# A corner of 64x64 triangular inverses: its first product moved from TensorE into VectorE's substitution

## The chip, the cores and the metric

One Trainium2 chip, of which the kernel uses one core. The metric is device time in microseconds of one execution of the whole layer, as the median of several runs. The engines are named as the profile names them: PE is TensorE (matmuls), DVE is VectorE, ACT is ScalarE, POOL is GpSimd, SP is SyncE, from which nearly all DMAs are issued.

## The reference

One layer of a hybrid encoder over 256 frames of width 4096, in float32. A projection of x feeds 16 heads of forgetting attention ("fox"), 32 heads of RWKV-7 time mixing (64 wide), and a gate; the gated outputs go through an output projection and a layer norm.

```python
proj = jnp.einsum('bsd,dc->bsc', x, w_in)
...
def frame_step(state, inp):
    r_t, w_t, k_t, v_t, a_t, b_t = inp
    sa = jnp.einsum('bhvk,bhk->bhv', state, a_t)
    state = (state * w_t[:, :, None, :] + sa[..., None] * b_t[:, :, None, :]
             + v_t[..., None] * k_t[:, :, None, :])
    return state, jnp.einsum('bhvk,bhk->bhv', state, r_t)
...
h = jnp.concatenate([fox_out, rwkv_out], axis=-1) * jax.nn.silu(z.astype(f32))
out = jnp.einsum('bsc,cd->bsd', h.astype(x.dtype), w_out)
x = _layernorm(ALPHA * x.astype(f32) + out.astype(f32), ln_gain, ln_bias, LN_EPS).astype(x.dtype)
```

The recurrence over frames is what the change touches. The kernel doesn't step through frames: it takes chunks of 64 frames (four of them), and inside a chunk the frames' influence on each other is the inverse of a unit triangular 64x64 matrix, one for each head and chunk.

## The kernel before, in words

**The main stream.** The two big projections run on PE as matmuls of 128x128 weights by 512 columns. Each float32 weight tile (128 x 1024) is loaded to `wr` (six buffers) and split into a rounded part, made by ACT (`wh`, four buffers), and the rest, made by DVE (`wl`, three buffers); lines 519 to 524. A tile of weights gives 12 matmuls: two pieces, two halves of the frames, three products each. First come 32 blocks of the input projection (n = 0 to 7 groups of two columns of heads, b = 0 to 3; lines 1311 to 1344), then eight blocks of the output projection (lines 1346 to 1392). Its first 32 weight tiles run on those heads that are already done (`begun`, line 600); then come the tiles 14 and 15 of block 0, which need the last heads' h, among them three that are not stored to memory and read back but kept in the tile `hl`.

**The side work.** While the main stream runs, generators (`prepare`, `rwkv`, `fox`, `unload`) are advanced one step after every second matmul triple (`slot`, line 592). `rwkv(n)` (line 918) does the time mixing of group n, that is four heads (two columns u, two halves j of the partitions) by four chunks c:

- `gp`: the products of the keys and receptances, masked into `gb` (the chunk's matrices, line 951) and `lt`.
- The 32x32 diagonal blocks of the triangular matrices are written to DRAM (`nd`) and read back spread over all partitions (`Nb`, line 955).
- The solve (lines 989 to 1001): DVE inverts all 32x32 blocks by back substitution, 31 steps of one product (`prod`) and one reduction (`xc`). A partition holds four columns (NJ = 4) of an inverse for each u; the width of a step grows from 1 to 31.
- The results go to DRAM (`td`) and come back as `T`, with blocks on their own partitions (lines 1002 to 1007); DVE transposes them into the diagonal of X (line 1026).
- The corner of each 64x64 inverse is a product of three 32x32 matrices. PE makes the first product `qt` from `gb` and T (lines 1027 to 1032, 16 matmuls, each two passes, 32 in the profile's count), ACT and DVE copy it to Q, and PE makes the second, `xp`, from Q and X (lines 1054 to 1059); ACT and DVE copy that into X.
- For each chunk: residual `rh`, solution `up`, state `sp` (lines 1068 to 1095), then the readout `yp` (lines 1096 to 1101): for each chunk and u, state SV by `lt` plus UV by `gb`, for both halves.
- `post`, norm and gate follow, and give h, which is stored or kept.

**What sets the order.** No engine's order is written by hand. `Later` (line 216) collects all operations with a modelled duration (`span_of`, line 149), and `flush` (line 274) runs them through a model of the five engines: each engine takes the ready operation with the lowest key, which is its place in the program, less 100000 for weight loads and splits (line 634). The order in the model becomes the program's order on each queue, and the engines then run in that order, waiting on semaphores. An operation counts as ready in the model some time after those that it depends on: `seen` (line 407) adds a margin of 1000 ns where PE depends on another engine, 1.5 times that behind a DMA and 0.15 times that otherwise (the margin is given with the flush, line 1374). `places` (line 418) looks whether the buffers of an operation's tiles are free in the model, and from when.

**Constants.** `cs` holds the 128x128 identity (C_ID), the masks, the right-hand sides of the solve (C_E) and others, for the whole run; the identity is needed in the end alone (lines 1381 and 1438).

Of the kernel before, what the change touches and what calls it, by code (L numbers as in the profile page):

```python
# [19 lines left out]
P = 128  # L20
S = 256
# [36 lines left out]
NJ = B // NG  # L58
C_ID = 0
C_MASK = 128  # L60
C_E = 256
C_SCAN = 384
C_ROW = C_SCAN + S
C_W = C_ROW + 2
LW = 2 * LORA + NF
# [26 lines left out]
MARGIN = 1000  # L92
APART = 2.4


# [120 lines left out]
class Later:  # L216
# [190 lines left out]
    def seen(self, o, op, margin):  # L407
        if o.engine == op.engine == "tensor":
            return o.start + o.hold
        if op.main or op.key < 0:  # L410
            return o.end
        if op.engine == "tensor":
            return o.end + margin
        if isinstance(o.lag, tuple):
            return o.end + margin * 1.5
        return o.end + margin * 0.15

    def places(self, op):
        at = 0.0
        for where in op.touches:  # L420
            if self.left[where][3]:
                continue
            free, queue = self.slots[self.left[where][0]]
            if not free or (len(free) < 5 and queue[0] != where and not self.left[where][0].startswith("ps")):
                return None
            at = max(at, free[0])
        return at
# [38 lines left out]
def layer(ctx: ExitStack, tc: tile.TileContext, xt, xtok, w_first, w_main, muv, w_o, up, par, mulora, fbias, lng, lnb, cst, out):  # L466
# [11 lines left out]

    cs = const.tile([P, C_W], F32, name="cs")
    prm = const.tile([P, len(PAR), G], F32, name="prm")  # L480
# [29 lines left out]
    nc.sync.dma_start(out=fb, in_=fbias)  # L510
    nc.sync.dma_start(out=cs, in_=cst)
    nc.earliest = 0

    ident = cs[:, C_ID : C_ID + P]

# [402 lines left out]
    def rwkv(n):  # L918
# [29 lines left out]
        for u in range(2):  # L948
            for j in range(2):
                h = HALF[j]  # L950
                nc.vector.tensor_tensor(gb[j][h, u], gv[u][j][h], m(h), ALU.mult)
            for a in range(4):
                o = B * (a % 2)
                nc.sync.dma_start(out=nd[u, a].rearrange("c r s -> r c s"), in_=gb[a // 2][B * a : B * (a + 1), u, :, o : o + B])
            nc.sync.dma_start(out=flat(nb[:, u]), in_=nd[u].rearrange("q c r s -> (q c) (r s)").unsqueeze(1).to_broadcast([16, NG, B * B]))
        for u in range(2):
            for j in range(2):
                o = HALF[1 - j]
                nc.vector.tensor_tensor(lt[j][o, u], parted(gv[u][j][o]), parted(m(o)), ALU.mult)
        states = rp.tile([P, 2, 2, NCH, C], F32, tag="SV", name=f"SV{n}")  # L960
        inputs = rp.tile([P, 2, 2, NCH, C], F32, tag="UV", name=f"UV{n}")
        SV, UV = ([t[:, j] for j in range(2)] for t in (states, inputs))
        yield from wait(W["tp"])
        for u in range(2):
            nc.vector.transpose(flat(BK[:, u]), flat(BK[:, u]))
        yield from wait(W["d1"])
        BKt = rp.tile([P, 2, NCH, P], F32, tag="shl", name=f"BKt{n}")
# [20 lines left out]
        other = turns()  # L988
        prod = rp.tile([P, 2, NJ, B], F32, tag="prod", name=f"prod{n}")
        xc = rp.tile([P, 2, NJ, B], F32, tag="xc", name=f"xc{n}")  # L990
        ev = cs[:, C_E : C_E + P].rearrange("p (j s) -> p j s", s=B)
        for u in range(2):
            nc.scalar.copy(prod[:, u], ev)
            nc.scalar.copy(xc[:, u, :, B - 1 : B], ev[:, :, B - 1 : B])
        for t, s in enumerate(range(B - 2, -1, -1)):
            w = B - 1 - s
            nc.vector.tensor_tensor(prod[:, :, :, s + 1 :], nb[:, :, s : s + 1, s + 1 :].to_broadcast([P, 2, NJ, w]), xc[:, :, :, s + 1 :], ALU.mult)
            nc.vector.tensor_reduce(xc[:, :, :, s : s + 1], prod[:, :, :, s:], AX.X, ALU.add)
            next(other, None)
            if t % ROWS == ROWS - 1:  # L1000
                yield
        td = dram.tile([2, 4, NCH, B, B], F32, tag="td", name=f"td{n}", bufs=2)
        T = rp.tile([P, 2, NCH, B], F32, tag="prod", name=f"T{n}")
        for u in range(2):
            nc.sync.dma_start(out=td[u].rearrange("q c (g j) s -> (q c g) (j s)", g=NG), in_=flat(xc[:, u]))
            for a in range(4):
                nc.sync.dma_start(out=T[B * a : B * (a + 1), u], in_=td[u, a].rearrange("c r s -> r c s"))
        vm = rp.tile([P, 2, 2, 2], F32, tag="vm", name=f"vm{n}")
# [14 lines left out]
        for a in range(4):  # L1023
            o = C * (a // 2) + B * (a % 2)
            rows = slice(B * a, B * (a + 1))
            nc.vector.transpose(X[rows].rearrange("p u c t -> p (u c) t")[:, :, o : o + B], T[rows].rearrange("p u c s -> p (u c) s"))
        qp = pst(f"qt{n}")
        for u in range(2):
            for c in range(NCH):
                for j in range(2):  # L1030
                    a, b = slice(C * j, C * j + B), slice(C * j + B, C * j + C)
                    nc.tensor.matmul(qp[b, u * P + c * B : u * P + (c + 1) * B], gb[j][a, u, c, B:C], T[a, u, c, :], start=True, stop=True)
        Q = rp.tile([P, 2, NCH, B], F32, tag="xc", name=f"Q{n}")
        for j in range(2):
            b = slice(C * j + B, C * j + C)
            (nc.vector.tensor_copy if j else nc.scalar.copy)(Q[b].rearrange("p u c s -> p (u c s)"), qp[b, : 2 * P])

        def residual(c):
# [13 lines left out]

        yield from wait(W["xp"])
        xp = pst(f"xp{n}")
# [42 lines left out]
        for c in range(NCH):  # L1097
            for u in range(2):
                for lhs, rhs in ((SV, [t[:, :, :, 1] for t in lt]), (UV, [t[:, :, :, C:P] for t in gb])):
                    for j in (1, 0):  # L1100
                        nc.tensor.matmul(yp[HALF[j], u * S + c * C : u * S + (c + 1) * C], lhs[j][:, u, c, :], rhs[j][:, u, c], start=lhs is SV, stop=lhs is UV)
        yield
# [245 lines left out]
    for b, q in outs:  # L1348
# [22 lines left out]
        if b == 0:  # L1371
            while sides:
                slot()
            nc.flush([t for _, *hl in ready for t in hl] + [raw for _, raw in raws], "_rp", MARGIN)
            mid.close()
            rpool = ctx.enter_context(tc.tile_pool(name="rpool", bufs=1))
            res = [rpool.tile([P, D], F32, tag=f"res{m}", name=f"res{m}") for m in range(2)]
            rows = rpool.tile([P, D], F32R, name="rows")
            nc.gpsimd.memset(rows.bitcast(F32), 0.0)
            identr = rpool.tile([P, P], F32R, name="identr")  # L1380
            nc.vector.tensor_copy(identr, ident)
            for n in range(2):
                load_tok(n)
            lbias = rpool.tile([P, OB], F32, name="lbias")
            lminus = rpool.tile([P, OB], F32, name="lminus")
            lneps = const.tile([P, 1], F32, name="lneps")
            nc.vector.memset(lneps, LN_EPS)
# [178 lines left out]
```

## Time and profile before

| | |
|---|---|
| runs before | 1906.97, 1906.69, 1906.51 us; median 1906.69 |
| the profiled execution | 1905.37 us; its span 1903.3 us |
| granted PE clock, mean | 0.999 |
| DVE, ACT, POOL busy | 1397.9, 970.8, 41.0 us |
| DMA | 443.89 MB in 349377 packets, 233 GB/s |
| qt of the eight groups, from the first to the last | 238.1 to 1555.1 us |
| yp, likewise | 272.1 to 1590.8 us |

Such rows are read so: engine, operation, the tile that it writes and those that it reads, partitions x elements, the count, then busy time and the mean duration of one, then the idle time of that engine just ahead of them and what ended it. In the rows of the timeline the first number is the start and the second the length, in us from the span's start. All operations have line 371, since the planner issues them there, so groups are told apart by tiles. Matmuls are pipelined: one begins while the one before it still runs, so the distance of two starts says what one costs.

### The profile page before, as it was taken

What the parts mean: (1) busy time and instruction counts of PE and PEld (TensorE: products, weight loads), DVE (VectorE), ACT (ScalarE), POOL (GpSimd) and SP (SyncE); (2) the same over time, 40 slices, a digit from 0 to 9 for tenths busy, and PEclk for the clock granted to TensorE, in tenths of its full rate; (3) what the DMA queues carried; (4) which work ended last, traced back from release to release, by engine and by line L of the source; (5) the groups of instructions that cost most, each with busy time, mean ns of one, the idle gap of its engine ahead of it and who ended that gap; (6) DMA issues with size and microseconds to landing.
All of it is one profiled execution on the core that took longest, in us unless ns stands there. A gap on an engine that the chain in (4) does not pass through costs nothing.

```text
span 1903.3 us, 28152 instructions
## 1 busy us (share of the span) xinstructions
PE 1894.5 (100%) x9882; PEld 1584.0 (83%) x9882; DVE 1397.9 (73%) x2413; ACT 970.8 (51%) x1488; POOL 41.0 (2%) x90
## 2 busy tenths in 40 slices
PE   9999999999999999999999999999999999999998
PEld 9988888888888888888888888888888888888887
DVE  6597778876887698769866986698669765765555
ACT  6464465445544554455445544554455444443342
POOL 0000000000000000000000000000000000000000
PEclk9999999999999999999999999999999999999999
DMA  9678877986897679777977798679767995966663
GB/s 349 212 220 261 228 206 241 262 225 193 241 261 227 199 233 265 229 199 229 270 226 198 234 264 225 195 239 267 225 196 231 340 306 174 318 206 200 190 197 144
DMA packets 349377, 443.89 MB, mean 233 GB/s; under 512 B 213666, under 2 KB 250116, under 8 KB 349236
## 3 DMA queue, kind: packets, MB, share of 16 engines
q1 hardware_dynamic: 348948, 441.73, 77.4%
q8 instruction: 77, 1.26, 0.3%
q14 instruction: 64, 0.52, 0.1%
q10 hardware_dynamic: 288, 0.37, 0.1%
HBM read 403.64 MB, written 38.36 MB: 232 GB/s over the span
## 4 chain that ended last, share of the span: by engine, by line
PE 99%; DVE 0%; DMA 0%; ACT 0%; issue 0%; DVEq 0%; SPq 0%; POOL 0%; ACTq 0%; POOLq 0%
PE acc L371 73%; PE oacc L371 18%; PE accl L371 2%; PE yp L371 1%; PE gp L371 1%; PE rh L371 1%; PE up L371 1%; PE lp L371 1%; PE sp L371 1%; PE fop L371 0%; PE fsp L371 0%; DMA fq<-bt 0%; PE side L371 0%; PE qt L371 0%; PE xp L371 0%; PE warmup L371 0%
## 5 line engine op out<-in xcount | busy, mean ns | idle before, releaser
L371 PE MATMUL acc<-w_1h,x 128*128 128x512 f32 x248 | 78.7, 394 | 0.0
L371 PE MATMUL acc<-w_0h,x 128*128 128x512 f32 x248 | 78.4, 393 | 0.2 <-ACT vt L371 0.2
L371 PE MATMUL acc<-w_8h,x 128*128 128x512 f32 x248 | 78.1, 392 | 0.0
L371 PE MATMUL acc<-w_5h,x 128*128 128x512 f32 x248 | 78.0, 392 | 0.0
L371 PE MATMUL acc<-w_15h,x 128*128 128x512 f32 x248 | 77.7, 394 | 0.0
L371 PE MATMUL acc<-w_13h,x 128*128 128x512 f32 x248 | 77.5, 392 | 0.0
L371 PE MATMUL acc<-w_10h,x 128*128 128x512 f32 x248 | 77.4, 393 | 0.0
L371 PE MATMUL acc<-w_9h,x 128*128 128x512 f32 x248 | 77.3, 392 | 0.0
L371 PE MATMUL acc<-w_14h,x 128*128 128x512 f32 x248 | 77.1, 391 | 0.0
L371 PE MATMUL acc<-w_3h,x 128*128 128x512 f32 x248 | 77.1, 392 | 0.0
L371 PE MATMUL acc<-w_11h,x 128*128 128x512 f32 x248 | 77.0, 392 | 0.0
L371 PE MATMUL acc<-w_12h,x 128*128 128x512 f32 x248 | 76.9, 391 | 0.0
L371 PE MATMUL acc<-w_2h,x 128*128 128x512 f32 x248 | 76.8, 390 | 0.0
L371 PE MATMUL acc<-w_6h,x 128*128 128x512 f32 x248 | 76.4, 389 | 0.0
L371 PE MATMUL acc<-w_4h,x 128*128 128x512 f32 x248 | 76.4, 389 | 0.0
L371 PE MATMUL acc<-w_7h,x 128*128 128x512 f32 x248 | 76.3, 389 | 0.0
L371 DVE TENSOR_REDUCE xc<-prod 128x8 f32<-128x16 f32 (+30 forms) x248 | 72.3, 291 | 5.5
L371 DVE TENSOR_TENSOR prod<-Nb,xc 128x8 f32<-128x8 f32 (+30 forms) x248 | 71.5, 288 | 6.3 <-DMA Nb<-nd 2.3
L371 DVE TENSOR_TENSOR w_7l<-w,w_7h 128x1024 fp32r<-128x1024 f32 x31 | 38.1, 1228 | 33.4 <-PE acc L371 31.2
L371 DVE TENSOR_TENSOR w_8l<-w,w_8h 128x1024 fp32r<-128x1024 f32 x31 | 38.0, 1225 | 31.2 <-PE acc L371 29.4
L371 ACT CAST w_11h<-w 128x1024 fp32r<-128x1024 f32 x31 | 32.7, 1055 | 48.6 <-PE acc L371 40.8
L371 ACT CAST w_10h<-w 128x1024 fp32r<-128x1024 f32 x31 | 32.7, 1055 | 47.2 <-PE acc L371 36.3
(652 smaller groups left out, 5451.6 us busy)
## 6 DMA issues: line engine op xcount, KB each, us to landing
w<-in_w_main_dram SPq DMA_DIRECT2D x496, 512.0 KB
wo<-in_w_o_dram SPq DMA_DIRECT2D x128, 512.0 KB
bt<-bk SPq DMA_DIRECT2D x96, 128.0 KB
fr<-in_w_first_dram SPq DMA_DIRECT2D x14, 720.0 KB
Nb<-nd SPq DMA_DIRECT2D x16, 512.0 KB
hd<-hl SPq DMA_DIRECT2D x29, 256.0 KB
h<-hd SPq DMA_DIRECT2D x29, 256.0 KB
raw<-bt SPq DMA_DIRECT2D x16, 256.0 KB
```

The costliest lines, as they stand in the source:

```text
L371: ins = op.call(*op.args, **op.kwargs)
```

## The change

1. **The corner's first product in the solve.** The off-diagonal 32x32 blocks of `gb` are transposed by DVE (`gt`), written to DRAM (`zd`) and read into the upper half of `prod`, which is twice as wide (2 NJ = 8 columns in place of four; the rest of that half is set to zero by POOL). They are right-hand sides of the same substitution: its 31 steps run over eight columns, and give, beside the inverses, the first products. These go through DRAM (`qd`) to Q, as the inverses go through `td` to T; T and Q now lie in one tile `TQ`, and T is loaded by four DMAs in place of eight. qt and its copies are gone, and so are the three steps of waiting ahead of xp.
2. **yp of chunk 0.** The state before the first chunk is zero in one half. ACT copies `lt` of chunk 0 into the half of `gb` that is otherwise zero, and the matmuls of SV for chunk 0 are left out: UV by `gb` does both.
3. **The identity** is no longer a part of `cs`, but is loaded to a tile of its own when the side work is done.
4. **The planner.** `seen` adds no margin where both operations are on the same engine (PE behind PE had none already). `places` lets an operation that writes a weight split (`wh`, `wl`) start no sooner than HOLD_OFF = 700 ns after its buffer is free, and counts several new tiles of one tag in one operation. The flush ahead of the output projection's second block keeps the accumulators of other blocks as taken.

```diff
-C_ID = 0
-C_MASK = 128
-C_E = 256
-C_SCAN = 384
+C_MASK = 0
+C_E = 128
+C_SCAN = 256
 C_ROW = C_SCAN + S
-C_W = C_ROW + 2
+C_ID = C_ROW + 2
+C_W = C_ID + P
...
+HOLD_OFF = 700
...
-        return o.end + margin * 0.15
+        return o.end + margin * 0.15 * (o.engine != op.engine)
...
-        at = 0.0
-        for where in op.touches:
-            if self.left[where][3]:
+        at, taken = 0.0, {}
+        for where in dict.fromkeys(op.touches):
+            tag, _, _, opened = self.left[where]
+            if opened:
                 continue
...
-            at = max(at, free[0])
+            at = max(at, free[n] + (HOLD_OFF if tag[:2] in ("wh", "wl") and op.engine != "tensor" else 0))
...
-    nc.sync.dma_start(out=cs, in_=cst)
+    nc.sync.dma_start(out=cs, in_=cst[:, :C_ID])
...
+            if u:
+                gt = rp.tile([P, 2 * NCH, B], F32, tag="xc", name=f"gt{n}")
+                zd = dram.tile([2, 2, NCH, B, B], F32, tag="zd", name=f"zd{n}", bufs=2)
+                for j in range(2):
+                    a = slice(C * j, C * j + B)
+                    nc.vector.transpose(gt[a], gb[j][a].rearrange("p u c t -> p (u c) t")[:, :, B:C])
+                    nc.sync.dma_start(out=zd[j].rearrange("u c k s -> k (u c) s"), in_=gt[a])
             nc.sync.dma_start(out=flat(nb[:, u]), in_=nd[u].rearrange("q c r s -> (q c) (r s)").unsqueeze(1).to_broadcast([16, NG, B * B]))
...
+        for j in range(2):
+            o = HALF[1 - j]
+            nc.scalar.copy(gb[j][o, :, 0, C:P], lt[j][o, :, 0, 1])
...
+        prod = rp.tile([P, 2, 2 * NJ, B], F32, tag="prod", name=f"prod{n}")
+        nc.gpsimd.memset(prod[:, :, NJ:], 0.0)
+        for j in range(2):
+            nc.sync.dma_start(out=prod[C * j : C * j + B, :, NJ:].rearrange("p u k s -> p u (k s)"), in_=zd[j].rearrange("u c (g k) s -> (c g) u (k s)", g=NG))
...
-            nc.vector.tensor_tensor(prod[:, :, :, s + 1 :], nb[:, :, s : s + 1, s + 1 :].to_broadcast([P, 2, NJ, w]), xc[:, :, :, s + 1 :], ALU.mult)
+            nc.vector.tensor_tensor(prod[:, :, :, s + 1 :], nb[:, :, s : s + 1, s + 1 :].to_broadcast([P, 2, 2 * NJ, w]), xc[:, :, :, s + 1 :], ALU.mult)
             nc.vector.tensor_reduce(xc[:, :, :, s : s + 1], prod[:, :, :, s:], AX.X, ALU.add)
...
-        td = dram.tile([2, 4, NCH, B, B], F32, tag="td", name=f"td{n}", bufs=2)
-        T = rp.tile([P, 2, NCH, B], F32, tag="prod", name=f"T{n}")
-        for u in range(2):
-            nc.sync.dma_start(out=td[u].rearrange("q c (g j) s -> (q c g) (j s)", g=NG), in_=flat(xc[:, u]))
-            for a in range(4):
-                nc.sync.dma_start(out=T[B * a : B * (a + 1), u], in_=td[u, a].rearrange("c r s -> r c s"))
+        td, qd = (dram.tile([4, 2, NCH, B, B], F32, tag=t, name=f"{t}{n}", bufs=2) for t in ("td", "qd"))
+        TQ = rp.tile([P, 2, 2 * NCH, B], F32, tag="prod", name=f"TQ{n}")
+        T, Q = (TQ[:, z].rearrange("p (u c) s -> p u c s", u=2) for z in range(2))
+        for d, cols in ((td, slice(0, NJ)), (qd, slice(NJ, 2 * NJ))):
+            for u in range(2):
+                nc.sync.dma_start(out=d[:, u].rearrange("q c (g j) s -> q (c g) (j s)", g=NG), in_=flat(xc[:, u, cols]))
+        for a in range(4):
+            nc.sync.dma_start(out=TQ[B * a : B * (a + 1), 0], in_=td[a].rearrange("u c r s -> r (u c) s"))
+        for j in range(2):
+            nc.sync.dma_start(out=TQ[C * j + B : C * j + C, 1], in_=qd[2 * j].rearrange("u c k s -> k (u c) s"))
...
-        qp = pst(f"qt{n}")
-        for u in range(2):
-            for c in range(NCH):
-                for j in range(2):
-                    a, b = slice(C * j, C * j + B), slice(C * j + B, C * j + C)
-                    nc.tensor.matmul(qp[b, u * P + c * B : u * P + (c + 1) * B], gb[j][a, u, c, B:C], T[a, u, c, :], start=True, stop=True)
-        Q = rp.tile([P, 2, NCH, B], F32, tag="xc", name=f"Q{n}")
-        for j in range(2):
-            b = slice(C * j + B, C * j + C)
-            (nc.vector.tensor_copy if j else nc.scalar.copy)(Q[b].rearrange("p u c s -> p (u c s)"), qp[b, : 2 * P])
...
-        yield from wait(W["xp"])
...
-                for lhs, rhs in ((SV, [t[:, :, :, 1] for t in lt]), (UV, [t[:, :, :, C:P] for t in gb])):
+                for lhs, rhs in ((SV, [t[:, :, :, 1] for t in lt]), (UV, [t[:, :, :, C:P] for t in gb]))[not c :]:
...
-            nc.flush([t for _, *hl in ready for t in hl] + [raw for _, raw in raws], "_rp", MARGIN)
+            nc.flush([t for _, *hl in ready for t in hl] + [raw for _, raw in raws] + [t for n in oacc if n for t in oacc[n]], "_rp", MARGIN)
...
+            ident = rpool.tile([P, P], F32, name="ident")
+            nc.sync.dma_start(out=ident, in_=cst[:, C_ID:])
             nc.vector.tensor_copy(identr, ident)
```

More of the change, by code (lines that the diff above doesn't have):

```diff
@@ L415, in seen @@
             return o.end + margin * 1.5
-        return o.end + margin * 0.15
+        return o.end + margin * 0.15 * (o.engine != op.engine)
     def places(self, op):
-        at = 0.0
-        for where in op.touches:
-            if self.left[where][3]:
+        at, taken = 0.0, {}
+        for where in dict.fromkeys(op.touches):
+            tag, _, _, opened = self.left[where]
+            if opened:
                 continue
-            free, queue = self.slots[self.left[where][0]]
-            if not free or (len(free) < 5 and queue[0] != where and not self.left[where][0].startswith("ps")):
+            free, queue = self.slots[tag]
+            n = taken[tag] = taken.get(tag, -1) + 1
+            if len(free) <= n or (len(free) < 5 and queue[n] != where and not tag.startswith("ps")):
                 return None
-            at = max(at, free[0])
+            at = max(at, free[n] + (HOLD_OFF if tag[:2] in ("wh", "wl") and op.engine != "tensor" else 0))
         return at
@@ L477, in pst @@
         return ps.tile([P, 512], F32, tag="ps", name=name)
-    cs = const.tile([P, C_W], F32, name="cs")
+    cs = const.tile([P, C_ID], F32, name="cs")
     prm = const.tile([P, len(PAR), G], F32, name="prm")
@@ L510, in layer @@
     nc.sync.dma_start(out=fb, in_=fbias)
-    nc.sync.dma_start(out=cs, in_=cst)
+    nc.sync.dma_start(out=cs, in_=cst[:, :C_ID])
     nc.earliest = 0
-    ident = cs[:, C_ID : C_ID + P]
     def column(name, i):
@@ L988, in rwkv @@
         other = turns()
-        prod = rp.tile([P, 2, NJ, B], F32, tag="prod", name=f"prod{n}")
-        xc = rp.tile([P, 2, NJ, B], F32, tag="xc", name=f"xc{n}")
+        xc = rp.tile([P, 2, 2 * NJ, B], F32, tag="xc", name=f"xc{n}")
         ev = cs[:, C_E : C_E + P].rearrange("p (j s) -> p j s", s=B)
         for u in range(2):
-            nc.scalar.copy(prod[:, u], ev)
-            nc.scalar.copy(xc[:, u, :, B - 1 : B], ev[:, :, B - 1 : B])
+            nc.scalar.copy(prod[:, u, :NJ], ev)
+            nc.scalar.copy(xc[:, u, :, B - 1 : B], prod[:, u, :, B - 1 : B])
         for t, s in enumerate(range(B - 2, -1, -1)):
             w = B - 1 - s
-            nc.vector.tensor_tensor(prod[:, :, :, s + 1 :], nb[:, :, s : s + 1, s + 1 :].to_broadcast([P, 2, NJ, w]), xc[:, :, :, s + 1 :], ALU.mult)
+            nc.vector.tensor_tensor(prod[:, :, :, s + 1 :], nb[:, :, s : s + 1, s + 1 :].to_broadcast([P, 2, 2 * NJ, w]), xc[:, :, :, s + 1 :], ALU.mult)
             nc.vector.tensor_reduce(xc[:, :, :, s : s + 1], prod[:, :, :, s:], AX.X, ALU.add)
@@ L1098, in rwkv @@
             for u in range(2):
-                for lhs, rhs in ((SV, [t[:, :, :, 1] for t in lt]), (UV, [t[:, :, :, C:P] for t in gb])):
+                for lhs, rhs in ((SV, [t[:, :, :, 1] for t in lt]), (UV, [t[:, :, :, C:P] for t in gb]))[not c :]:
                     for j in (1, 0):
-                        nc.tensor.matmul(yp[HALF[j], u * S + c * C : u * S + (c + 1) * C], lhs[j][:, u, c, :], rhs[j][:, u, c], start=lhs is SV, stop=lhs is UV)
+                        nc.tensor.matmul(yp[HALF[j], u * S + c * C : u * S + (c + 1) * C], lhs[j][:, u, c, :], rhs[j][:, u, c], start=lhs is SV or not c, stop=lhs is UV)
         yield
```

## The prediction

> **What bounds the kernel now.** I read the first page first (busy time, then the chain that ended last), then the waits of TensorE, then the busy time of one group's stretch.
>
> ```profile
> span 1903.3 us, 28152 instructions
> PE 1894.5 (100%) x9882; PEld 1584.0 (83%) x9882; DVE 1397.9 (73%) x2413; ACT 970.8 (51%) x1488; POOL 41.0 (2%) x90
> PE 99%; DVE 0%; DMA 0%; ACT 0%; issue 0%; DVEq 0%; SPq 0%; POOL 0%; ACTq 0%; POOLq 0%
> ```
> ```profile
> PE sp L371 <- ACT UV L371: 1.0, 1, 1.0
> ```
> ```profile
> 390.00:579.30 189.30, 189.30 (x1010) 157.31 (x1009) 145.59 (x265) 100.42 (x160) 4.44 (x9) 1.00 0.81 231
> ```
> TensorE is busy all but 8.8 us of the span, its longest wait is one of 1.0 us, and the chain that ended last is TensorE for 99%. The last row is one group (two columns of heads; there are eight): its columns are PE, PEld, DVE, ACT, POOL, granted clock, DMA share and GB/s. PE fills all 189.3 us, at full clock. So what leaves PE leaves the time, one for one, as long as nothing makes PE wait. DVE has 43.7 us free in a group, ACT 88.9 us, POOL nearly all. The profiled execution took 1905.37 us: its span and 2.07 us around it, 1.32 us less than the median of the runs, 1906.69.
>
> **What leaves PE.** Two things: the product qt, and the SV half of yp for the first chunk.
>
> ```profile
> L371 PE MATMUL yp<-lt,SV 128*64 128x64 f32 x256 | 15.8, 225 | 0.0
> L371 PE MATMUL qt<-T,gb 32*32 32x32 f32 x256 | 5.5, 192 | 0.0
> ```
> ```profile
> 237.29 0.39 PE L371 MATMUL acc<-w_12l,x 128*128 128x512 f32 x1
> 237.52 0.61 PE L371 MATMUL acc<-w_12h,x 128*128 128x512 f32 x2
> 238.07 0.69 PE L371 MATMUL qt<-T,gb 32*32 32x32 f32 x32
> 238.69 0.50 PE L371 MATMUL acc<-w_12l,x 128*128 128x512 f32 x1
> 239.03 0.62 PE L371 MATMUL acc<-w_12h,x 128*128 128x512 f32 x2
> 239.49 0.40 PE L371 MATMUL acc<-w_12l,x 128*128 128x512 f32 x1
> ```
> Matmuls overlap, so the price is read from starts, not from busy time. In the undisturbed rhythm (237.29 to 237.52) one weight matmul follows another by 0.23 us. From 237.52 to 239.03 three weight matmuls start; they are worth 0.69 us and it took 1.51. So a qt costs 0.82 us: 0.62 for its own 32 passes (238.07 to 238.69) and 0.20 at its edges. Eight of them: 6.6 us.
>
> ```profile
> 272.25 0.29 PE L371 MATMUL yp<-gb,UV 128*64 128x64 f32 x4
> 272.37 0.29 PE L371 MATMUL yp<-lt,SV 128*64 128x64 f32 x4
> 272.48 0.29 PE L371 MATMUL yp<-gb,UV 128*64 128x64 f32 x4
> ```
> The rows of yp (256 passes of the SV half in eight groups, so 32 a group) start 0.115 us apart, four passes each. For chunk 0 both SV rows go (u = 0 and 1): 2 x 0.115 x 8 = 1.9 us. No edge is won here, since yp stays. The UV half takes over the work of the missing one by two ACT copies of lt into the empty half of gb, far ahead of yp. Nothing new runs on PE. Sum: 6.6 + 1.9 = 8.5 us.
>
> **What DVE gets.** The substitution has 31 steps of a product and a reduction, and each is now twice as wide.
>
> ```profile
> L371 DVE TENSOR_REDUCE xc<-prod 128x8 f32<-128x16 f32 (+30 forms) x248 | 72.3, 291 | 5.5
> L371 DVE TENSOR_TENSOR prod<-Nb,xc 128x8 f32<-128x8 f32 (+30 forms) x248 | 71.5, 288 | 6.3 <-DMA Nb<-nd 2.3
> ```
> ```profile
> L371 DVE STREAM_TRANSPOSE X<-T 32x256 f32<-32x256 f32 x32 | 13.9, 435 | 0.8
> L371 DVE TENSOR_TENSOR prod<-Nb,xc 128x248 f32<-128x248 f32 x8 | 3.3, 416 | 0.2
> L371 DVE TENSOR_REDUCE xc<-prod 128x8 f32<-128x256 f32 x8 | 3.3, 415 | 0.0
> L371 DVE TENSOR_TENSOR prod<-Nb,xc 128x8 f32<-128x8 f32 x8 | 1.4, 172 | 2.3 <-DMA Nb<-nd 2.3
> L371 DVE TENSOR_REDUCE xc<-prod 128x8 f32<-128x16 f32 x8 | 1.1, 140 | 0.1
> ```
> From 8 to 248 elements a product grows from 172 to 416 ns, 1.02 ns an element; a reduction from 140 to 415 ns over 240 elements, 1.15. Step w adds 8w elements to the product and 8(w+1) to the reduction; over w = 1 to 31 that is 3968 and 4216 elements, so 4.0 + 4.8 = 8.9 us a group on top of today's 18.0 (143.8 in eight groups). The two transposes into gt add 2 x 0.435 us, and the copy of Q that goes saves about as much as one. So DVE takes some 9.3 us more of the 43.7 us that it has free: PE is not overtaken. ACT wins and loses copies of a few tenths of a us, POOL gets a memset; both have the room shown above.
>
> **Where it becomes later.** The solve is a chain, and on the way to yp. In one solve:
>
> ```profile
> 353.00:400.70 47.70, 41.26 (x94) 1.00 0.87 255
> ```
> ```profile
> 365.27 1.22 DVE L371 TENSOR_TENSOR w_8l<-w,w_8h 128x1024 fp32r<-128x1024 f32 x1 [0.49 <-PE acc L371]
> 367.30 0.27 DVE L371 TENSOR_REDUCE xc<-prod 128x8 f32<-128x112 f32 x1
> 367.99 1.23 DVE L371 TENSOR_TENSOR w_9l<-w,w_9h 128x1024 fp32r<-128x1024 f32 x1 [0.42 <-PE acc L371]
> ```
> ```profile
> 373.63 0.39 PE L371 MATMUL acc<-w_9l,x 128*128 128x512 f32 x1
> ```
> The first row (DVE alone) says: 41.3 us of work in 47.7, 6.4 us idle. The weight splits take 1.23 us in every 2.72, 45%, so what doesn't fit the idle time costs 1.82 us for each us of work. If all the idle time is filled, the solve gets (8.9 - 6.4) x 1.82 = 4.5 us longer; if none, 16.2. I take 6, near the low end, by the bracketed 0.42 and 0.49 us: DVE stands in front of a split whose buffer PE still reads, with the next step queued behind. HOLD_OFF plans each split 0.7 us later, so that steps go ahead of it. Besides, the planner no longer adds 0.15 us between two dependent steps on one engine; 62 steps times 0.15 us are 9.3 us of planned gaps, about what the wider steps add, so the planned order hardly stretches. A split that starts 0.7 us later still has cover: w_9l is done at 369.22 and first read at 373.63, 4.4 us later.
>
> The rest of that way:
>
> ```profile
> 241.18 0.69 PE L371 MATMUL xp<-X,Q 32*32 32x32 f32 x32
> ```
> ```profile
> 406.64 2.25 SPq L371 DMA_DIRECT2D T<-td  x3
> 410.33 3.28 SPq L371 DMA_DIRECT2D T<-td  x4
> 414.14 0.43 SPq L371 DMA_DIRECT2D T<-td  x1
> ```
> xp stands 3.1 us behind qt (238.07 to 241.18); of that, four transposes of X (1.7 us) are still needed, so 0 to 1.4 us is won; I take 0.5. SP issues 14 DMAs a group in place of 10 (zd and the load into prod ahead of the solve, qd and Q behind it; T in four in place of eight), past weight loads that are queued there. The eight T loads (128 pieces of 128 bytes each) took SP 7.9 us. zd writes and Q reads have as many pieces again, half of them behind the solve: 0 to 4.0 us ahead of it and 0 to 4.0 behind; I take 0.5 each, since T needs only half as many issues and zd goes while Nb is under way. So yp moves by 6 - 0.5 + 1 = 6.5 us (3.1 to 24.2).
>
> Who waits for that? In groups 0 to 6 nobody on PE. In the last group h does:
>
> ```profile
> 1621.88 0.42 DVE L371 TENSOR_TENSOR hl<-h,hl 128x256 fp32r<-128x256 f32 x1 [0.47 <-ACT hl L371]
> ```
> ```profile
> 1630.53 0.61 PE L371 MATMUL oacc<-wo_15h,hl 128*128 128x512 f32 x2
> ```
> The last hl is ready at 1622.30 and wo_15 needs it at 1630.53: 8.2 us of cover. The need comes 1.1 us sooner in the new kernel (this group's own qt and yp rows), so 7.2 are left, and the 6.5 us stay under it by 0.7. The move of ident to a tile of its own puts one load ahead of the identr cast in DVE's queue at the same place, and the splits behind it have the 4.4 us of lead as cover; I count it at nothing, or at most (that cover gone) the 1.0 us of the wait shown above. At most that 1.0 us is won back, too, if the wait on UV goes.
>
> By this the profiled execution would be 1905.37 - 8.5 = 1896.9 us, the median of the runs 1906.69 - 8.5 = **1898.2**; with the wait of 1.0 us lost or won, 1897.2 to 1899.2.
>
> **A rule against it.** The page's count of small packets says how common such pieces already are:
>
> ```profile
> DMA packets 349377, 443.89 MB, mean 233 GB/s; under 512 B 213666, under 2 KB 250116, under 8 KB 349236
> ```
> The change adds 1024 pieces of 128 bytes a group, 8192 in all, 4% of the 213666. The Trainium skill, "DMA: Bandwidth & Descriptors", section Specifications, says that transfers under 512 bytes don't run at line rate, since the engine reads, modifies and writes. By that rule the time would be the one of rival 2. No row here has the price of one such piece by itself, so the trace doesn't decide it.
>
> **The rivals.** (1) The late tail: the solve uses little of DVE's idle time and stretches by 9 to 16 us. For it: fixed queue order, DVE waits for PE in it. Against: the planned gaps that go. yp moves 9.5 to 16.5 us, PE stands 2.3 to 9.3 us before wo_15: 1900.5 to 1907.5; 1901.5 at 10.5 us.
> (2) Slow small pieces: zd and Q cost SP and the queue what T's cost, 4.0 us on each side of the solve. yp moves 6 - 0.5 + 8.0 = 13.5 us, PE waits 6.3: 1904.5. Against: the eight T loads are mostly spaced out by weight loads between them.
> (3) Slower: splits starve PE at the end of each solve. A step of the last dozen takes up to 0.67 + 0.71 us (416 + 248 x 1.02; 415 + 256 x 1.15). A tile of weights leaves DVE 2.72 - 1.23 = 1.49 us: two operations fit, three (2.06) don't, and the split comes 0.57 us later each time. Over eight tiles that is 4.6 us, just the lead of 4.4. With four between splits (2.75 us, six tiles) it is 7.6 us: PE would wait 3.2 us in each group, 25.6 in all, 1923.8. It turns slower once a group loses more than 1.5 us. Against: splits come first in the planner.
> (4) The change doesn't return qt's edges, because xp's group takes them over: 8 x 0.62 + 1.9 = 6.9 us, 1899.8.
>
> **How the numbers follow.** The forecast has 0.60, the late tail 0.17, the small pieces 0.06, starved splits 0.10, lost edges 0.07. A measurement of this kernel can tell about 0.2%, 3.8 us: faster is under 1902.9, slower above 1910.5. Forecast, lost edges and two thirds of the late tail are faster (0.78); the rest of the tail, the small pieces and half of the starved splits are the same (0.17); 0.05 are slower. The range goes from 1896.5, a little under the forecast's own low end, to 1905.0, which takes in rivals 2 and 4 and most of 1; starved splits and the long end of the tail stay out, some 0.15.
>
> **What would show it.** Right: no qt, 192 passes of the SV half of yp, PE's idle time still near 9 us, the product at 496 elements near 0.67 us, a solve of 52 to 56 us, hl ready some 1 us ahead of wo_15, and DVE near 1472 us. Wrong: a wait of PE for hl or h in the row of waits (rivals 1, 2), waits of weight matmuls for DVE's splits in every group (3), or weight matmuls still set back beside xp by more than now (4).

## The result, and the profile after

The changed kernel takes **1894.88 us** (median of five runs, 1894.52 to 1898.45), the kernel before 1906.97 (five runs, 1906.51 to 1908.25) in the same series: ratio 0.9938 [0.9926, 0.9949], or 9.7 to 14.1 us less. The forecast was 1898.2, its range 1896.5 to 1905.0: the sign was right, but the result lies 1.6 us below the low end. The profiled execution of the changed kernel took 1894.52 us, its span 1892.7.

The first page of the changed kernel:

```profile
span 1892.7 us, 27577 instructions
PE 1885.3 (100%) x9562; PEld 1577.5 (83%) x9562; DVE 1452.0 (77%) x2421; ACT 975.0 (52%) x1496; POOL 41.3 (2%) x98
DMA packets 360913, 446.49 MB, mean 236 GB/s; under 512 B 222002, under 2 KB 261652, under 8 KB 360772
```

TensorE still fills the span but for 7.4 us (8.8 before). All waits of TensorE in it that are long enough for the view:

```profile
PE warmup L372 <- POOL idle L372: 1.0, 1, 1.0
PE accl L372 <- ACT wf1h L372: 0.4, 1, 0.4
PE wp L372 <- ACT l L372: 0.2, 1, 0.2
```

The wait of sp for UV is gone, none came for a weight split, and none for h or hl. The substitution, in the groups of instructions:

```profile
L372 DVE TENSOR_TENSOR prod<-Nb,xc 128x16 f32<-128x16 f32 (+30 forms) x248 | 104.8, 423 | 13.6 <-ACT xc L372 7.9
L372 DVE TENSOR_REDUCE xc<-prod 128x16 f32<-128x32 f32 (+30 forms) x248 | 107.5, 434 | 4.5
```

104.8 + 107.5 against 71.5 + 72.3: 68.5 us more, 8.6 a group. One group to the next, read from the first matmul of the same weight tile in two consecutive groups of the changed kernel:

```profile
841.21 0.62 PE L372 MATMUL acc<-w_7h,x 128*128 128x512 f32 x2
...
1029.40 0.62 PE L372 MATMUL acc<-w_7h,x 128*128 128x512 f32 x2
```

1029.40 - 841.21 = 188.19 us. The same two starts lie 189.24 apart in the kernel before: a group is 1.05 us shorter.

The end of the side work in the changed kernel, in the timeline of VectorE and of TensorE:

```profile
1611.03 0.42 DVE L372 TENSOR_TENSOR hl<-h,hl 128x256 fp32r<-128x256 f32 x1
```
```profile
1620.51 0.62 PE L372 MATMUL oacc<-wo_15h,hl 128*128 128x512 f32 x2
```

The last hl is ready at 1611.45, 10.85 us sooner than before; wo_15 reads it 10.02 us sooner. The cover, 8.2 us before, is 9.1 now. The forecast had it down to 0.7.

### The profile page after: what moved, and what is told of

It is laid out like the page before. It is cut to its first block, busy times and chain, and to the rows that moved or that the text cites. A ratio compares the mean times of both kernels' runs of the same rounds, so it can differ in the third digit from the quotient of the medians.

```text
span 1892.7 us, 27577 instructions
## 1 busy us (share of the span) xinstructions
PE 1885.3 (100%) x9562; PEld 1577.5 (83%) x9562; DVE 1452.0 (77%) x2421; ACT 975.0 (52%) x1496; POOL 41.3 (2%) x98
## 2 busy tenths in 40 slices
DMA packets 360913, 446.49 MB, mean 236 GB/s; under 512 B 222002, under 2 KB 261652, under 8 KB 360772
## 4 chain that ended last, share of the span: by engine, by line
PE 99%; DVE 0%; DMA 0%; DVEq 0%; issue 0%; SPq 0%; ACT 0%
PE acc L372 73%; PE oacc L372 18%; PE accl L372 2%; PE gp L372 1%; PE yp L372 1%; PE rh L372 1%; PE up L372 1%; PE lp L372 1%; PE sp L372 1%; PE fop L372 1%; PE fsp L372 0%; PE side L372 0%; PE xp L372 0%; DMA fr<-in_w_first_dram 0%; DVE res L372 0%; PE wp L372 0%
## 5 line engine op out<-in xcount | busy, mean ns | idle before, releaser
L372 DVE TENSOR_TENSOR prod<-Nb,xc 128x16 f32<-128x16 f32 (+30 forms) x248 | 104.8, 423 | 13.6 <-ACT xc L372 7.9
L372 DVE TENSOR_REDUCE xc<-prod 128x16 f32<-128x32 f32 (+30 forms) x248 | 107.5, 434 | 4.5
L372 ACT CAST w_6h<-w 128x1024 fp32r<-128x1024 f32 x31 | 32.6, 1053 | 46.8 <-PE acc L372 43.7
L372 ACT CAST w_7h<-w 128x1024 fp32r<-128x1024 f32 x31 | 32.7, 1054 | 43.3 <-PE acc L372 39.9
L372 PEld LDWEIGHTS acc<-w_0h,x 128*128 128x128 f32 x248 | 46.6, 188 | 10.0 <-DVE vx L372 0.4
```

The source lines that it names most:

```text
L372: ins = op.call(*op.args, **op.kwargs)
```

## The experiments

The theory to test, A: TensorE's passes set the time, 1.05 us in each of eight groups, and everything else is cover that holds or doesn't. Its rivals: the new order of the queues wins by itself; the wider solve is nearly out of cover; the wait of sp for UV is worth more than the 1.0 us of one execution. In each diff the lines with a minus belong to the kernel named. Each ratio is to the kernel before, run in between on the same chip. There were three such series on three chips, in which the kernel before has medians of 1907.68, 1908.18 and 1908.86 us, so times of different series are best compared by their ratios.

### The order of the queues alone

The kernel before, with part 4 of the change (`seen`, `places`, the flush) and nothing else.

```diff
+HOLD_OFF = 700
...
-        return o.end + margin * 0.15
+        return o.end + margin * 0.15 * (o.engine != op.engine)
...
-            at = max(at, free[0])
+            at = max(at, free[n] + (HOLD_OFF if tag[:2] in ("wh", "wl") and op.engine != "tensor" else 0))
...
```

> The kernel before with the planner's edits alone (HOLD_OFF, no margin on the same engine, the places and the flush of after); qt, yp and the narrow solve stay. Theory A (PE time): nothing leaves PE, so the eight groups keep their 189.2 us each; at most the one wait of 1.0 us in the last group (sp for UV) goes. Time 1905.9 to 1907.0 us. Theory B (order): the new queues win the 3.6 us by which the change beat the forecast (12.1 instead of 8.5), with no matmul removed: about 1903.4 us, and groups shorter by some 0.4 us.

1908.14 us; ratio 0.9995 [0.9985, 1.0004]: no difference that can be told, a gain of 2.9 us at most. The waits of TensorE:

```profile
PE qt L372 <- DMA T<-td: 1.3, 1, 1.3
PE oacc L372 <- ACT bk L372: 0.5, 1, 0.5
```

The wait of sp is gone and two others have come. The order alone wins nothing in time. But it shortens the solve a lot, from 48.0 to 50.0 us to 35.1 to 36.8, of which more below.

### The edit of yp alone

The kernel before, with the two copies of lt into gb and the shorter list for chunk 0.

```diff
+            nc.scalar.copy(gb[j][o, :, 0, C:P], lt[j][o, :, 0, 1])
...
-                for lhs, rhs in ((SV, [...]), (UV, [...])):
+                for lhs, rhs in ((SV, [...]), (UV, [...]))[not c :]:
```

> The kernel before with only the SV half of yp for chunk 0 left out (lt copied into gb by ACT). Theory A: 64 of 512 passes go, 0.23 us a group, 1.9 us in all: 1905.1 us, each group 188.95 to 189.0 us. Rival: the passes of SV and UV overlap, so that a missing row of four returns less than the 0.115 us between starts: under 1 us in all, 1906 us or more.

1907.59 us; ratio 0.9993 [0.9982, 1.0004]. Inconclusive: 1.9 us are 0.9990, inside an interval that also holds 1. In the trace the groups without a stall are 189.04 us apart (189.24 before), 0.2 us less as the rows of yp said. But sp waits longer than in the first profile, and two more waits have come:

```profile
PE sp L371 <- ACT UV L371: 2.0, 1, 2.0
PE acc L371 <- ACT vt L371: 1.2, 4, 0.6
PE fsp L371 <- DVE qx L371: 1.0, 1, 1.0
```

### qt made twice

The kernel before, with the 16 matmuls of qt issued a second time right behind the first, into the same places.

> The kernel before with the 32 passes of qt issued twice in one group of matmuls (the second time overwrites the first with the same values). Theory A with edges paid once per group: 32 more passes cost 0.50 to 0.62 us a group, 4.0 to 5.0 us in all: 1911.0 to 1912.0 us. If the 0.20 us of edges belonged to the passes themselves: 0.82 us a group, 6.6 us: 1913.6 us. If small matmuls hid under the weight matmuls: under 1 us.

1912.09 us; ratio 1.0024 [1.0012, 1.0035], 4.4 us more by the medians. The groups are 189.82 us apart: 0.58 us for 32 more passes whose edges are paid already.

### The changed kernel once more

> The changed kernel once more, for a second profile. Theory A: each group again 1.05 us shorter than before, no wait of sp for UV in the last group, and what is left of the 12.1 us (the end behind the last matmul, 11.4 us against 11.9, and the difference between the profiled execution and the median) is spread between executions: the end anywhere from 11.3 to 11.9 us, the median 1894.5 to 1896 us. Theory B says nothing else here.

1895.14 us (five runs); ratio 0.9937 [0.9924, 0.9950]. The result stands. The groups without a stall are 188.2 us apart again. This profiled execution, at 1898.07 the slowest of its five, has three waits that the first one doesn't show:

```profile
PE fsp L372 <- DVE kx L372: 1.1, 1, 1.1
PE acc L372 <- ACT bk L372: 0.8, 1, 0.8
PE xp L372 <- DMA TQ<-qd: 0.5, 1, 0.5
```

So single waits of about a microsecond come and go between executions of one program.

### One load planned later

What does sp wait for? The timeline of ScalarE in the kernel before, last group:

```profile
1562.01 0.42 ACT L371 ACTIVATE fq<-fq 128x256 f32<-128x256 f32 x1 [2.72 <-DMA fq<-bt]
...
1563.55 1.03 ACT L371 CAST wo_0h<-wo 128x1024 fp32r<-128x1024 f32 x1
1564.48 0.53 ACT L371 COPY UV<-up 64x128 f32<-64x128 f32 x2
```

The bracket says that the scaling of fq, work of a fox head, stood 2.72 us for its load. The copy of UV, which needs nothing from it, stood behind it in the same queue, and TensorE behind the copy. The last matmul of up, which UV copies, ends at about 1561.5: some 0.5 us of the wait for the load held UV up directly, and the rest of its delay is the work between the two, which came late with the scaling. In the changed kernel UV is copied at 1550.80, ahead of that scaling. The experiment is the kernel before, in which the planner takes the last fox head's loads to land 4 us later, so that UV goes first:

```diff
+        if self.late:
+            op.lag = op.lag[0], op.lag[1] + self.late, op.lag[2]
...
+            nc.late = 4000 * (i == G - 1)
             issue(t, d[4 * j : 4 * j + 4].rearrange("b i m a t -> (b i) (m a t)"))
+            nc.late = 0
```

> The kernel before, with one change to the plan alone: the four loads of the last fox head count as landing 4 us later, so that in ACT's queue the copies of UV (first chunk of the last group) stand ahead of the scaling of fq, which waits for its load. Nothing leaves PE. Theory C: the forecast was beaten because the kernel before loses 1.2 to 2.8 us in the last group, where PE (sp) waits for UV behind fq, and the changed kernel does not. Then this wait is gone, no other takes its place, and the time falls by 1 to 3 us: 1904.7 to 1906.7 us against 1907.7 of before. Rival D: the waits are scattered and others (T, bk) come in its place, as in the kernel with the planner's edits alone: 1907.7 us, within 0.5.

1906.43 us against 1908.18; ratio 0.9987 [0.9978, 0.9996]: 0.8 to 4.2 us less, 1.75 by the medians. No wait of sp is left in its trace. So taking this wait away wins time, and by the medians more than the 1.0 us of the first profile; the interval reaches down to 0.8, so that it is more is likely and not shown.

### The changed kernel with an order near the old one

The changed kernel with HOLD_OFF = 0 and a margin of 100 ns between operations of one engine (150 in the kernel before; that full margin wasn't tried with the wider solve).

```diff
-HOLD_OFF = 700
+HOLD_OFF = 0
...
-        return o.end + margin * 0.15 * (o.engine != op.engine)
+        return o.end + margin * (0.15 if o.engine != op.engine else 0.1)
```

> The changed kernel with HOLD_OFF = 0 and a margin of 100 ns between operations on the same engine (150 before, 0 after). The corner and yp as after. Theory A and C: the PE time stays won, UV still stands ahead of fq in ACT's queue; the solve stretches from 51 to 53 us to 56 to 62 us, which the cover of the last group takes (hl ready 9.1 us ahead of wo_15 in the changed kernel). Time 1894.9 to 1897 us. Theory B: the order is worth the 3.6 us: 1898.7 us. Rival of the late tail: PE waits for hl by more than 1 us: 1897 us or more.

1907.76 us; ratio 0.9997 [0.9989, 1.0006]. All of the gain is gone, a larger loss than I expected of it. Waits of TensorE, then the busy time of VectorE in the last group's solve:

```profile
PE acc L372 <- DVE vx L372: 4.4, 6, 1.1
PE oacc L372 <- ACT hl L372: 2.1, 1, 2.1
PE xp L372 <- DMA TQ<-qd: 1.6, 1, 1.6
```
```profile
1494.00:1552.90 58.90, 52.09 (x97) 1.00 1.05 355
```

The solve leaves 6.8 us idle and takes 58.9 (56.9 to 58.9 in the eight groups), the last hl is ready at 1635.46, and TensorE waits 2.1 us for one of the last three. That is the late tail of the prediction, and beside it stands a wait for vx, six times, that no rival had.

### The corner without the edit of yp

The changed kernel with the two copies and the shorter list taken back.

> The changed kernel with the SV half of yp for chunk 0 back (and the two ACT copies gone). Theory A: 0.23 us more a group, 1.9 us in all: 1897.0 us, groups of 188.45 us in place of 188.2. If overlapped passes return less than their distance of starts: 1895.1 to 1896 us.

1899.48 us; ratio 0.9953 [0.9940, 0.9965], 4.6 us above the changed kernel's first median. The groups are 188.45 us apart, 0.26 more than with the edit, which makes 2.1 us in eight; the profile has also one wait of 1.1 us (oacc for the split wo_13l). In the clean groups, then, yp's term is what the rows said. The rest of the 4.6 isn't in the groups: that wait is a part of it, and so is the change of series, since against the kernel before beside it this kernel gains 8.7 us, and the changed kernel gained 12.1 and 12.5.

### A longer last solve

The changed kernel, with the product of each step of the last group's solve made twice: 13.1 us more for VectorE (an eighth of the 104.8 us above).

```diff
+            if n == G // 2 - 1 and w > 0:
+                nc.vector.tensor_tensor(prod[:, :, :, s + 1 :], nb[:, :, s : s + 1, s + 1 :].to_broadcast([P, 2, 2 * NJ, w]), xc[:, :, :, s + 1 :], ALU.mult)
```

> The changed kernel with each of the 31 products of the last group's solve made twice (same values): 13.1 us more of DVE work on the way to the last h, nothing more on PE. Theory of the forecast (only the last group's h has a reader on PE that can wait, behind 9.1 us of cover): the solve stretches by 13.1 to 23.8 us, and PE waits 4 to 14.7 us near wo_14 and wo_15: 1899 to 1910 us. Rival: the average share of DVE counts and the tail is hidden anyway: 1895 to 1896 us. With the changed kernel's own cover far larger than 9 us (other work moves ahead of it on PE), the same.

1911.18 us; ratio 1.0017 [1.0007, 1.0026]. The last solve takes 77.3 us instead of 50.6 (first product to last reduction): 26.7 more, twice the work that was added (the prediction's factor for a solve without idle time to fill, 1.82, makes 23.8). The wait of TensorE, and TensorE's busy time and granted clock in stretches ahead of it and behind it:

```profile
PE oacc L372 <- ACT hl L372: 11.9, 1, 11.9
```
```profile
1617.60:1619.60 2.00, 2.00 (x9) 1.00 0.79 219
1631.60:1633.60 2.00, 2.00 (x5) 0.50 0.00 0
```

So a solve that ends late does end the time, through hl, and the wait is paid with more than its length: see the last section.

### Which edit of the planner makes the fit

The changed kernel with HOLD_OFF = 0 alone (no margin between operations of one engine, as in the changed kernel), and with the margin of 100 ns on one engine alone.

> The changed kernel with HOLD_OFF = 0 and nothing else altered (the margin of 100 or 150 ns stays). Theory A, the two planner edits share the fit: solves of 53 to 57 us, one or two waits of acc for vx or of oacc for hl of 1 to 2 us, 1897 to 1904. Theory B, HOLD_OFF alone makes the fit: this run looks like e6, solves of 57 to 60 us, waits of acc for vx of 4 us, 1905 to 1909. Theory C, the margin alone makes it: solves of 51 to 53 us, no wait over 1 us, 1894 to 1897.

1903.25 us; ratio 0.9977 [0.9967, 0.9987].

```profile
PE xp L372 <- DMA TQ<-qd: 3.6, 9, 0.6
PE acc L372 <- ACT vt L372: 1.9, 6, 0.5
```

The solves are as short as in the changed kernel (50.7 to 52.9 us), as theory C had it, but the time is theory A's. What is late now is a transfer: in the fifth group the last reduction ends at 971.52, the issues of TQ's loads run from 977.85 to 987.11, and xp starts at 989.64; in the changed kernel the reduction ends at 965.59, they run from 970.88 to 978.64, and xp starts at 983.26. So the last load is issued 15.6 us behind the solve instead of 13.1.

> The changed kernel with the same-engine margin back at 100 ns and HOLD_OFF left at 700. Theory A: solves of 53 to 57 us, 1897 to 1904. Theory B, HOLD_OFF alone makes the fit: solves of 51 to 53 us, the last hl read at about 1620 us, 1894 to 1897. Theory C, the margin alone makes it: solves of 57 to 60 us, the last hl at 1629 us or later and a wait of oacc for it of about 2 us, 1905 to 1909.

1924.37 us; ratio 1.0083 [1.0065, 1.0102], beyond every expectation.

```profile
PE oacc L372 <- ACT hl L372: 17.1, 1, 17.1
PE oacc L372 <- ACT bk L372: 4.7, 1, 4.7
```

The matmuls of gp, with which the last group begins, start at 1487.6 us (1457.8 in the changed kernel), its solve at 1518.3 (1479.4), and it takes 59.7 us (50.6); TensorE's wait for hl ends at 1645.1. The four orders of the changed kernel side by side, from three series, with the ratio to the kernel before in each:

| | margin 100 ns on one engine | no margin on one engine |
|---|---|---|
| HOLD_OFF 0 | 1907.76 (0.9997) | 1903.25 (0.9977) |
| HOLD_OFF 700 | 1924.37 (1.0083) | 1894.88 (0.9938) |

Neither edit is a gain with a size of its own: HOLD_OFF costs some 16 us with the margin and wins 7 to 8 without it. Each gives another order, and the order decides which cover fails.

### qt left out

The kernel before without qt, its copies and Q; xp multiplies T in Q's place, so the corner's first product is left out of the computation.

```diff
-        qp = pst(f"qt{n}")
...
-                    nc.tensor.matmul(xp[a, u * P + c * B : u * P + (c + 1) * B], Q[b, u, c, :], X[b, u, c, C * j + B : C * j + C], start=True, stop=True)
+                    nc.tensor.matmul(xp[a, u * P + c * B : u * P + (c + 1) * B], T[b, u, c, :], X[b, u, c, C * j + B : C * j + C], start=True, stop=True)
```

> The kernel before with qt, its two copies and Q left out, and xp multiplying T in Q's place: this leaves out part of the computation and adds nothing to VectorE. Theory A, the whole step between the neighbours of the group returns, 0.82 us x 8 = 6.6 us, and the wait of sp for UV stays, because the scaling that waits for fq still stands ahead of it: about 1901 us, groups of 188.4 us in the trace. Theory B, only the 32 passes return and the edges stay: 0.62 x 8 = 5.0 us, about 1902.5 us, groups of 188.65. Theory C, the shorter chain to the last hl frees a wait that no view shows: under 1898 us.

1898.23 us against 1908.86; ratio 0.9947 [0.9928, 0.9966], 6.5 to 13.7 us less. Two starts of the same weight tile, one group apart, and the wait:

```profile
842.29 0.61 PE L371 MATMUL acc<-w_7h,x 128*128 128x512 f32 x2
...
1030.71 0.62 PE L371 MATMUL acc<-w_7h,x 128*128 128x512 f32 x2
```
```profile
PE sp L371 <- ACT UV L371: 2.1, 1, 2.1
```

188.42 us, 0.82 less than before: in the groups the passes and the edges both return, as theory A has it. (188.4 was expected, 188.65 without the edges.) With 0.58 for the passes from qt made twice, the edges are 0.24. In the time it is less clear. The median falls by 10.6 us where theory A has 6.6, and lies close to theory C's 1898; the interval just reaches 6.6. The wait of sp is still there in the profile, so nothing shows that the 4.0 us beyond theory A are that wait; but the profiled execution, 1900.58 us, is the second longest of the six, and the others have no profile.

### The kernel before once more

> The kernel before once more, for a second profile of it. Theory A, the first profiled execution was a lucky one with a short wait: sp waits for UV again, 1.2 to 2.8 us, and the profiled execution lies above 1905.4, by the wait that it has more. Theory B, the wait of sp was an accident of that execution: none over 0.5 us at sp now, and other waits in its place. Theory C: all waits as in the first profile to 0.2 us, and the distance to the median lies outside the waits of TensorE.

1909.10 us (12 runs, ratio 0.9999 [0.9987, 1.0010]), the profiled execution 1908.49.

```profile
PE sp L371 <- ACT UV L371: 2.7, 1, 2.7
```

Theory A: sp waits again, 1.7 us longer than in the first profile, and the execution is 3.1 us longer. Five profiles of kernels with fq ahead of UV show this wait: 1.0, 2.0, 2.6, 2.1 and 2.7 us, 2.1 in the mean. The one that the forecast was built on is the shortest.

## Why the prediction was right in direction and too cautious in size

**What leaves PE: right.** qt's 0.82 us a group is 0.82 (qt left out); the two yp rows' 0.23 is 0.20 to 0.26; together 1.05 forecast, 1.05 measured, 8.4 us over eight groups where the sum said 8.5. The rival of the lost edges is refuted. In the changed kernel nothing stands around xp that did not stand there before:

```profile
606.31 0.61 PE L372 MATMUL acc<-w_9h,x 128*128 128x512 f32 x2
606.85 0.69 PE L372 MATMUL xp<-X,TQ 32*32 32x32 f32 x32
607.48 0.45 PE L372 MATMUL rh<-SV,lt 128*64 128x64 f32 x8
607.86 0.50 PE L372 MATMUL acc<-w_9l,x 128*128 128x512 f32 x1
```

The second matmul of the first row starts at about 606.54; from there to the next weight matmul it is 1.32 us, and 1.33 around the same xp of the kernel before.

**What DVE gets: right to 4%.** 8.6 us a group where 8.9 was forecast; the widest product took 0.67 us as forecast. The busy total was forecast at 1472 and is 1452.0, because busy time counts overlapping instructions once: the summed durations rose by 70.6 us, the busy time by 54.1.

**The length of the solve: shorter than its low bound.** VectorE in the solves of the third and of the last group, from the first product to the last reduction, first before, then after:

```profile
539.95:589.40 49.45, 42.98 (x97) 1.00 0.89 255
1485.70:1535.80 50.10, 42.80 (x97) 1.00 1.06 371
```
```profile
536.40:588.85 52.45, 51.39 (x99) 1.00 0.86 251
1479.40:1530.00 50.60, 48.76 (x93) 1.00 1.05 372
```

In eight groups the solve took 48.0 to 50.0 us before, with 6.1 to 7.3 idle, and takes 50.6 to 52.9 now, with 1.0 to 1.9 idle: 2.3 to 3.3 us longer in groups 0 to 6 and 0.6 in the last, against 6 (4.5 to 16.2). The prediction added the wider steps to the old solve. The planner's edits alone show what they are added to, here in the third group's solve with the narrow steps:

```profile
541.90:577.65 35.75, 34.34 (x87) 1.00 0.88 260
```

The new order takes 11 to 14 us out of the narrow solve, idle time and the work of others, and leaves 1.4 to 2.8 us idle. From there the wider steps add 14.0 to 16.7 us a group, near the 16.2 that the prediction had for the case that none of the idle time is filled. It named the planned gaps that go ("62 steps times 0.15 us are 9.3 us") but took 6 us, near the low end, for the sum of both effects. Of the two edits it is the margin that makes the solve short: with HOLD_OFF = 0 the solves are as short, with the margin of 100 ns they take 54.1 to 59.7 us, HOLD_OFF or not.

**The way from the solve to xp: the wrong sign.** Forecast half a microsecond longer; in the last group it is 5 us shorter. The issues of SP, first in the kernel before, then in the changed one:

```profile
1535.79 0.57 SPq L371 DMA_DIRECT2D fpt<-lg  x1
1536.41 0.65 SPq L371 DMA_DIRECT2D bt<-bk  x1
1537.73 1.34 SPq L371 DMA_DIRECT2D wo<-in_w_o_dram  x1
1539.16 0.85 SPq L371 DMA_DIRECT2D td<-xc  x2
...
1551.25 0.43 SPq L371 DMA_DIRECT2D T<-td  x1
```
```profile
1530.03 1.23 SPq L372 DMA_DIRECT2D td<-xc  x2
...
1537.74 1.93 SPq L372 DMA_DIRECT2D TQ<-td  x4
...
1540.24 0.92 SPq L372 DMA_DIRECT2D TQ<-qd  x2
```

Before, the last reduction ended at 1535.78 and td was issued 3.4 us later, behind three other transfers; the last T was issued at 1551.25 and xp started at 1558.18. Now td follows the reduction at once (1529.99, 1530.03), six loads are issued by 1541.16, and xp starts at 1547.49: 22.4 us before, 17.5 now. In the other seven groups td was issued at once before, too, and the way is 0.5 to 1.8 us shorter. I had priced the new transfers and not the place of the old ones in the queue. With the shorter solve this made the cover of the last hl grow where the sum had it nearly used up. In the time it changed nothing, since TensorE waits there neither by the forecast nor in the run; it took the ground from the late tail.

**The small pieces.** The rule that I cited from the Trainium skill ("DMA: Bandwidth & Descriptors", section Specifications) decides nothing here: 8336 more packets under 512 bytes (222002 against 213666), and in the first profile TensorE waits for none of them. But its place is real: with HOLD_OFF = 0 TQ<-qd is what xp waits for in six of the eight groups, 3.6 us in all. The same loads are issued later there, as the times of the fifth group show; whether the pieces are also slow by themselves, no run here tells.

**The step that failed** is the last of the sum: "At most that 1.0 us is won back, too, if the wait on UV goes", and with it 1906.69 - 8.5 as the middle. The wait was read from one execution, itself 1.32 us under the median. In five profiles it is 2.1 us in the mean, and taking it away alone is worth about 1.75 us (0.8 to 4.2). With 8.4 + 2.1 = 10.5 the forecast would have been 1896.2 from the median then shown, and 1896.5 would not have been the low end. From the two first profiles the gain adds up nearly without rest: 8.4 by the groups, 1.3 at sp with its restart, 0.5 behind the last matmul, 0.4 in scattered places, together the 10.6 us between the spans. Of the 12.1 us between the medians some 1.5 stay unexplained. They lie within the interval (9.7 to 14.1) and within the scatter of the kernel before, whose runs went from 1903.6 to 1914.8 in one series.

That the wait of sp was sized too low is shown; that it is all of what was missed is not. With qt left out sp still waited, 2.1 us in the profile, and the median fell by 4.0 us more than what left TensorE. And the executions of the kernel before differ in their mean granted clock: of the 78 in the three series of experiments, the 51 at 0.999 or 1.000 took 1907.5 us in the mean, the 27 at 0.997 or 0.998 took 1910.6. The two groups are 0.0015 apart in the mean clock; by an estimate, 0.0015 of 1907 us is 2.9 us of time lost at half clock, which would be nearly all of these 3.1 us. The last section shows one wait of sp that cost clock. In the run with fq's loads planned later 1 execution of 11 lies below 0.999, against 11 of 29 of the kernel before beside it; of the changed kernel's ten, it is one. Which waits do it in the executions without a profile stays open.

**The rivals.** Late tail: not here, but real, and at the place where the prediction put it, the cover of the last hl: in the order near the old one, in the longer solve and with the margin of 100 ns. Starved splits: in none of these profiles does TensorE wait for a w split beside a solve; that the time with the margin of 100 ns and HOLD_OFF, 1924.37, is close to that rival's 1923.8 is chance, since its waits are for hl and bk.

## What to carry to other kernels

Where one engine fills the span, price what leaves it by the distance of starts, edges included: this came out to a few hundredths of a microsecond a group. But take the waits from several executions before bounding what they can give back, count the clock that a wait can cost with it, and look at what stands ahead of the late instruction on its own queue: here a scaling that waited for its load held up a copy that needed nothing from it. And where a planner makes the order, measure an edit together with the order that it brings: the same computation took between 1894.9 and 1924.4 us with two constants of the planner.

## What the runs showed of the hardware

A long wait of TensorE costs more than its length. Behind the wait of 11.9 us in the longer solve the granted clock was 0.50, and it returned late; TensorE's busy time and clock, further on:

```profile
1639.60:1640.60 1.00, 1.00 (x4) 0.50 1.05 365
1640.60:1641.60 1.00, 1.00 (x5) 0.83 1.02 268
1641.60:1642.60 1.00, 1.00 (x7) 1.00 1.00 320
```

The half clock lasted from 1631.6 to about 1640.9, some 9 us, in which matmuls started 0.43 us apart instead of 0.23: about 4.5 us lost on top of 11.9, and with a second wait of 0.7 us that makes nearly the whole 17.6 us by which this span is longer. The Trainium skill ("TensorE: Matmul & The Clock Gate", Part 1) has full clock return after some 3.4 us of sustained work. Behind the wait of 17.1 us with the margin of 100 ns and HOLD_OFF it did, after 3 to 4 us; in the longer solve it took nearly three times that, with a wait of 0.7 us in between, 4.6 us after the start.

A short wait can cost clock as well, but doesn't always. Behind the waits of 1.0, 2.0, 2.6 and 2.7 us at sp the granted clock stayed at 1.00, and the rows behind them keep 0.39 us a matmul. Behind the wait of 2.1 us at the same place, with qt left out, TensorE went on at 1559.84, and the clock was 0.50 from about 1560.6 to 1564.1:

```profile
1560.80:1563.80 3.00, 3.00 (x8) 0.50 0.78 229
1564.20:1566.20 2.00, 2.00 (x12) 1.00 0.23 86
```

Those 3.4 us at half clock are about 1.7 us lost, nearly as much as the wait. The same followed a wait of 1.6 us for TQ in the order near the old one (0.50 from about 1572.4 to 1575.8) and the wait of 4.7 us with the margin of 100 ns and HOLD_OFF (1529.3 to 1532.7). What decides whether a wait of 2 us does it, these runs don't show.
